# RWKV-7 scan products and second block-inverse products, issued in turn by head

## The chip, the cores and the metric

The kernel runs on one core of a Trainium2 chip. The metric is the device time of one execution in microseconds (us); lower is better. Before the change the median of three runs is 2846.87 us (2844.48 to 2854.17).

## The reference

Two layers of a hybrid generator run over 256 context and 256 latent tokens of width 2048. Each layer makes one input projection, sends it through four mixers in parallel (A: windowed attention, B: RWKV-7, C: global attention, D: gated DeltaNet), gates and merges them, and projects back. Cut to what the change touches:

```python
# the four mixers of a layer; B (RWKV-7) and D (gated DeltaNet) are the recurrent ones
p = h @ w_in;  pc = hc @ w_in
y_b, z_b = _mixer_b(p[..., OFF_B:OFF_C], pc[..., OFF_B:OFF_C], ...)
y_d, z_d = _mixer_d(p[..., OFF_D:OFF_G], pc[..., OFF_D:OFF_G], ...)
x = x + gate[:, None] * _merge([y_a, y_b, y_c, y_d], p[..., OFF_G:], g_up, g_b, w_br, w_out)

def _rwkv_scan(s0, r, w, k, v, kk, a, reverse):          # 8 heads of 64 channels, two directions
    def step(s, inp):                                    # one token
        r_t, w_t, k_t, v_t, kk_t, a_t = inp
        sa = jnp.einsum('bhij,bhj->bhi', s, -kk_t)
        s = (s * w_t[:, :, None, :] + sa[..., None] * (kk_t * a_t)[:, :, None, :]
             + v_t[..., None] * k_t[:, :, None, :])
        return s, jnp.einsum('bhij,bhj->bhi', s, r_t)
    s, y = lax.scan(step, s0, xs, reverse=reverse)

def _gdn_chunked(s0, q, k, v, lg, beta):                 # mixer D, chunks of 64 tokens
    t_mat = a_mat + jnp.eye(c)                           # unit lower triangular
    sol = lax.linalg.triangular_solve(t_mat, rhs, left_side=True, lower=True, unit_diagonal=True)
    ...
```

## The kernel before

**Tiling of the scan.** The kernel does not walk the RWKV recurrence by token. It cuts 512 tokens into eight chunks of 64 and writes a chunk's work as 64x64 matrix products in float32. Two heads are worked at a time (the loop over `j` in `mixer_b`, four pairs per layer). Head 0 of the pair lies in partitions 0 to 63, head 1 in partitions 64 to 127: `HS` in `b_scan`. A product of head 0 uses rows and columns 0 to 63 of TensorE's array and one of head 1 uses rows and columns 64 to 127. Below, a digit behind a letter is the head.

**One step of `b_scan`** (eight per direction and head pair, 128 in all) consists of, in the order of the code:

- Z: `a` = AT10 by vt and, from the second step on, `b` = ar by the state S, summed in one PSUM tile `sc`; DVE copies it to `Z`.
- U: `z` = the inverse block (tile `iR`) by Z; DVE copies it to `U`.
- S: `k` = tok1 by vt and `u` = tok0 by U, summed in one tile `sc`; DVE scales it into the new state `S` (not on the last step).
- y, where outputs are needed: `V` = vt by AT11, `s` = S by ar, `w` = U by AT01, summed in PSUM tile `acc`.

**Block inverses.** `inv_gen` inverts 64x64 unit triangular blocks. DVE solves 32x32 halves by substitution (tiles `it`, `iX`, then two transposes into `iE` and `iF`). TensorE then joins them by two sets of 32x32 products: the first set (`p1`, iF by iL) alternates between the two halves of the partitions already; the second (`p2`, iT by iE) goes through the list `out`. Each entry of `out` holds one half and four or eight blocks. It runs 24 times: 16 times for B with 16 second products, 8 times for D (`pair`) with 24.

**What sets the order.** Every matmul goes through `Kern.mm` (L283), which charges a planner's cost for it in `small`. When the debt is high enough the planner pumps the next portion of a queue of wide products into the program: input projections, modulation, merges (tiles `big`, weights `wh` and `wl` split by ACT at L375 and DVE at L312). So scan steps and wide products lie mixed on TensorE. The change alters no charged cost: a product costs by its own shape and by the form of the one before it. Last, a scheduler rearranges the recorded instructions of each engine before they become the program; TensorE then starts its list strictly in the order that stands there.

Of the kernel before, what the change touches and what calls it, by code (L numbers as in the profile page):

```python
# [187 lines left out]
class Kern:  # L188
# [515 lines left out]
    def inv_gen(s, pool, st, sign, grp, R, pair=False):  # L704

        nc = s.nc
        Bt, X, lo = st
        x = X.rearrange("p m i -> p i m")  # L710
        for k in range(31):
            n, w = 31 - k, k // 4 + 1
            tm = s.tl(pool, [128, 80], "it")[:, 0:n * w].rearrange("p (a b) -> p a b", a=n)
            b = Bt[:, k, k + 1:32].rearrange("p (a o) -> p a o", o=1).to_broadcast([128, n, w])
            s.tt(tm, b, x[:, k:k + 1, 0:w].to_broadcast([128, n, w]), ALU.mult)
            yield
            s.tt(x[:, k + 1:, 0:w], x[:, k + 1:, 0:w], tm, ALU.subtract if sign > 0 else ALU.add)
            yield
        fl = X.rearrange("p a b -> p (a b)")
        o4 = lambda z: z.rearrange("p u (m d) -> p m d u", d=4)  # L720
        E = s.tl(pool, [128, 8, 32], "iE")
        F = s.tl(pool, [128, 8, 32], "iF")
        nc.vector.transpose(o4(E), fl)
        yield
        nc.vector.transpose(F, E)

        for _ in range(6):
            yield
        ps = s.bank()
        p1 = ps[:, 0:256].rearrange("p (u c) -> p u c", u=8)  # L730
        p2 = ps[:, 256:512].rearrange("p (u c) -> p u c", u=8)
        T1 = s.tl(pool, [128, 8, 32], "iT")
        HQ = [(slice(64 * h, 64 * h + 32), slice(64 * h + 32, 64 * h + 64)) for h in range(2)]

        w = R.shape[2] - 64
        out = [(R, h, u0, u1, 0, wE) for u0, u1, wE in grp for h in range(2)]
        if pair:
            EX = s.tl(pool, [128, 4, 64], "iG")
            out += [(EX, 0, 0, 4, 0, True), (EX, 1, 4, 8, 4, False)]
        for u in range(8):  # L740
            for up, dn in HQ:
                s.mm(p1[up, u, :], lo[dn, u, :], F[dn, u, :])
        for up, dn in HQ:
            nc.scalar.copy(T1[up], p1[up])
        for D_, h, u0, u1, du, wE in out:
            up, dn = HQ[h]
            c = w * h if D_ is R else 0
            X_ = E if wE else F
            d = slice(u0 - du, u1 - du)
            nc.gpsimd.memset(D_[up, d, c + 32:c + 64] if wE else D_[dn, d, c:c + 32], 0.0)  # L750
            nc.gpsimd.tensor_copy(D_[up, d, c:c + 32], X_[up, u0:u1])
            nc.gpsimd.tensor_copy(D_[dn, d, c + 32:c + 64], X_[dn, u0:u1])
        yield
        for D_, h, u0, u1, du, wE in out:
            up, dn = HQ[h]
            for u in range(u0, u1):
                if wE:
                    s.mm(p2[dn, u, :], T1[up, u, :], E[up, u, :])
                else:
                    s.mm(p2[up, u, :], E[up, u, :], T1[up, u, :])  # L760
        for D_, h, u0, u1, du, wE in out:
            up, dn = HQ[h]
            c = w * h if D_ is R else 0
            d = slice(u0 - du, u1 - du)
            if wE:
                s.act(D_[dn, d, c:c + 32], p2[dn, u0:u1, :], AF.Copy, float(-sign))
            else:
                s.act(D_[up, d, c + 32:c + 64], p2[up, u0:u1, :], AF.Copy, float(-sign))
        if not pair:
            return  # L770
        yield
        H0, H1 = slice(0, 64), slice(64, 128)
        ps = s.bank((128, 8, 64))
        for u0, u1, wE in grp:
            f1 = EX[H1] if wE else R[H1, u0:u1, 64:128]
            for u in range(u0, u1):
                s.mm(ps[H0, u, :], R[H1, u, 0:64], f1[:, u - u0, :])
        T2 = s.tl(pool, [128, 8, 64], "iB")
        nc.scalar.copy(T2[H0], ps[H0])
        for u0, u1, wE in grp:  # L780
            nc.gpsimd.memset(R[H0, u0:u1, 64:128] if wE else R[H1, u0:u1, 0:64], 0.0)
        yield
        ps = s.bank((128, 8, 64))
        for u0, u1, wE in grp:
            for u in range(u0, u1):
                if wE:
                    s.mm(ps[H1, u, :], T2[H0, u, :], R[H0, u, 0:64])
                else:
                    s.mm(ps[H0, u, :], EX[H0, u - u0, :], T2[H0, u, :])
        for u0, u1, wE in grp:  # L790
            if wE:
                s.act(R[H1, u0:u1, 0:64], ps[H1, u0:u1, :], AF.Copy, float(-sign))
            else:
                s.act(R[H0, u0:u1, 64:128], ps[H0, u0:u1, :], AF.Copy, float(-sign))
# [176 lines left out]
    def b_scan(s, J, d):  # L971
        nc = s.nc
        pool, t0 = s.bst["pool"], s.bst["t0"]
        c0 = t0 // 64
        ar, AT, tok, E, wc = J["d"][d]
        vt = J["vt"]
        HS = (slice(0, 64), slice(64, 128))
        if d == 0:
            J["y"] = s.acc_bank()
        yps = J["y"]  # L980
        pc = None
        S = None
        for st in range(8):
            c = s.ORDER[d][st]
            ps = s.scb((128, 64))
            for R in HS:
                s.mm(ps[R, :], AT[1][0][R, c, :], vt[R, c, :], True, st == 0)
                if st > 0:
                    s.mm(ps[R, :], ar[R, c, 0, :], S[R, :], False, True)
            Z = s.tl(pool, [128, 64], "Z")  # L990
            nc.vector.tensor_copy(Z, ps)
            s.bgstep(BG[0])
            ps = s.scb((128, 64))
            for R in HS:
                s.mm(ps[R, :], E[R, c, :], Z[R, :])
            U = s.tl(pool, [128, 64], "U")
            nc.vector.tensor_copy(U, ps)
            s.bgstep(BG[1])
            Sn = None
            if st < 7:  # L1000
                ps = s.scb((128, 64))
                for R in HS:
                    s.mm(ps[R, :], tok[1][R, c, :], vt[R, c, :], True, False)
                    s.mm(ps[R, :], tok[0][R, c, :], U[R, :], False, True)
                Sn = s.tl(pool, [128, 64], "S")
                if st == 0:
                    s.ts(Sn, ps, wc[:, c:c + 1], None, ALU.mult)
                else:
                    sw = s.tl(pool, [128, 64], "sw")
                    s.act(sw, S, AF.Copy, wc[:, c:c + 1])  # L1010
                    s.stt(Sn, ps, wc[:, c:c + 1], sw, ALU.mult, ALU.add)
            if c >= c0:
                for R in HS:
                    o = yps[R, c * 64:c * 64 + 64]
                    s.mm(o, vt[R, c, :], AT[1][1][R, c, :], d == 0 and c == c0, False)
                    if st > 0:
                        s.mm(o, S[R, :], ar[R, c, 1, :], False, False)
                    s.mm(o, U[R, :], AT[0][1][R, c, :], False, d == 1 and st == 7)
            s.bgstep(BG[2])
            S = Sn  # L1020

# [579 lines left out]
```

## Time and profile before

| | |
|---|---|
| median of three runs | 2846.87 us |
| the profiled execution's own time | 2842.45 us |
| its span | 2840.7 us |
| TensorE matmul busy | 2710.4 us, 95% |
| DVE, ACT, GpSimd busy | 65%, 44%, 6% |
| TensorE's granted clock over the span | 0.984 |

An entry of the profile is one hardware instruction. A float32 product 64x64 or 32x32 leaves two matmul entries (two passes), and the entries of two products can overlap in time. The end of an entry is modelled, so the time that a stretch of small products takes is read from the start of its first entry to the start of the wide product that follows it.

### The profile page before, as it was taken

How to read it: one execution, taken by the hardware profiler on the slowest of the kernel's cores; microseconds unless marked ns; L12 is line 12 of the kernel's file. 1: busy time of each engine (PE TensorE's matmuls, PEld its weight loads, DVE VectorE, ACT ScalarE, POOL GpSimd, SP SyncE). 2: the span in 40 equal slices, each digit the busy share in tenths (PEclk: the TensorE clock that was granted, in tenths of full speed). 3: DMA queues.
4: the chain of work that ended last, by engine and by line, in shares of the span. 5: the costliest groups of instructions: out<-in, count | busy, mean ns of one | idle time of the engine just before them, and what ended most of it. 6: DMA issues, size and time to landing. Idle time of an engine off the chain costs nothing. (4 is left out here: it accounts for less than half of the span.)

```text
span 2840.7 us, 52626 instructions
## 1 busy us (share of the span) xinstructions
PE 2710.4 (95%) x19438; PEld 2056.8 (72%) x19438; DVE 1856.9 (65%) x5255; ACT 1260.0 (44%) x2705; POOL 180.0 (6%) x436
## 2 busy tenths in 40 slices
PE   7998999999999998999999999999999999999897
PEld 3676666677787786777787756776777887867897
DVE  4337776656676777876553354777765687678775
ACT  3334333333354555655442244444443356455553
POOL 0000000000010101000000000010010001100000
PEclk9999999999999999999999999999999999999999
DMA  9753243322342323224537886322332442433465
GB/s 346 261 189 127 83 131 105 127 83 68 115 121 88 100 72 115 79 82 134 170 114 248 279 282 203 96 78 78 93 91 75 157 143 88 133 98 88 144 190 159
DMA packets 210049, 385.80 MB, mean 136 GB/s; under 512 B 24640, under 2 KB 37824, under 8 KB 209792
## 3 DMA queue, kind: packets, MB, share of 16 engines
q1 hardware_dynamic: 199872, 351.23, 39.6%
q0 software_dynamic: 9920, 31.20, 2.9%
q8 instruction: 153, 2.51, 0.4%
q14 instruction: 104, 0.85, 0.1%
HBM read 346.95 MB, written 35.39 MB: 135 GB/s over the span
## 5 line engine op out<-in xcount | busy, mean ns | idle before, releaser
L283 PE MATMUL big<-Rb,wh 128*128 128x512 f32 (+1 forms) x3280 | 1100.7, 364 | 21.3 <-ACT Rb L1325 10.0
L283 PE MATMUL big<-Ra,wh 128*128 128x512 f32 (+1 forms) x2128 | 777.3, 365 | 8.9 <-DVE po L315 5.6
L375 ACT CAST wh<-wr 128x512 fp32r<-128x512 f32 x712 | 438.8, 619 | 762.8 <-PE big L283 576.2
L283 PEld LDWEIGHTS big<-Rb,wh 128*128 128x128 f32 x3280 | 612.1, 191 | 128.8 <-ACT Rb L1325 14.0
L312 DVE TENSOR_TENSOR wl<-wr,wh 128x512 fp32r<-128x512 f32 x712 | 488.4, 688 | 304.3 <-ACT wh L375 280.3
L283 PE MATMUL big<-Ra,wl 128*128 128x512 f32 (+1 forms) x1616 | 597.2, 370 | 6.3 <-DVE wl L312 6.3
L283 PEld LDWEIGHTS big<-Ra,wh 128*128 128x128 f32 x2128 | 407.5, 192 | 84.3 <-issue 9.5
L283 PE MATMUL big<-Rb,wl 128*128 128x512 f32 (+1 forms) x1088 | 380.4, 350 | 1.1 <-DVE wl L312 1.1
L283 PEld LDWEIGHTS big<-Ra,wl 128*128 128x128 f32 x1616 | 310.3, 192 | 53.4 <-DVE wl L312 8.6
L283 PEld LDWEIGHTS big<-Rb,wl 128*128 128x128 f32 x1088 | 207.6, 191 | 26.2 <-DVE wl L312 1.5
L312 DVE TENSOR_TENSOR iX<-iX,it 128x60 f32<-128x60 f32 (+24 forms) x744 | 181.4, 244 | 15.7
L312 DVE TENSOR_TENSOR it<-iB,iX 128x60 f32<-128x60 f32 (+24 forms) x744 | 172.7, 232 | 15.6
L315 DVE SCALAR_TENSOR_TENSOR po<-po,big 128x512 f32<-128x512 f32 (+1 forms) x128 | 70.6, 552 | 77.1 <-PE big L283 74.2
L283 PE MATMUL big<-Rb,wr 128*128 128x256 f32 (+1 forms) x448 | 111.3, 417 | 5.0 <-ACT po L309 3.1
L309 ACT ACTIVATE sw<-S,wc 128x64 f32<-128x64 f32 x96 | 33.4, 348 | 176.2 <-DVE S L315 153.5
L283 PE MATMUL big<-mr,s 128*32 128x512 f32 x384 | 85.2, 617 | 18.3 <-DMA mr<-in_wmod 18.3
L309 ACT ACTIVATE po<-big,gb 128x512 f32<-128x512 f32 (+1 forms) x128 | 74.2, 579 | 57.3 <-PE big L283 41.2
L283 PEld LDWEIGHTS big<-Rb,wr 128*128 128x128 f32 (+1 forms) x448 | 70.6, 179 | 24.1 <-issue 7.3
L283 PE MATMUL sc<-vt,AT 64*64 64x64 f32 x512 | 71.3, 238 | 0.0
L315 DVE SCALAR_TENSOR_TENSOR cz<-raw,par,cz 128x508 f32<-128x508 f32 (+3 forms) x96 | 67.2, 700 | 5.4 <-ACT cz L309 5.0
L632 DVE TENSOR_REDUCE mx<-mx 128x1 f32<-128x512 f32 (+1 forms) x96 | 57.1, 599 | 18.7 <-PE mx L283 17.5
L283 PE MATMUL sc<-vt,tok 64*64 64x64 f32 x448 | 67.5, 232 | 0.0
(371 smaller groups left out, 4033.0 us busy)
## 6 DMA issues: line engine op xcount, KB each, us to landing
wr<-in_win SPq DMA_DIRECT2D x440, 256.0 KB, 2.7
mr<-in_wmod SPq DMA_DIRECT2D x320, 256.0 KB, 5.0
wr<-in_wbr SPq DMA_DIRECT2D x128, 256.0 KB, 2.7
wr<-in_wout SPq DMA_DIRECT2D x128, 256.0 KB, 3.1
wr<-in_wmod SPq DMA_DIRECT2D x64, 256.0 KB, 3.9
wr<-in_gup SPq DMA_DIRECT2D x64, 256.0 KB, 2.6
x<-in_xT SPq DMA_DIRECT2D x16, 256.0 KB, 5.4
po<-y SPq DMA_DIRECT2D x16, 256.0 KB, 3.0
```

The lines of the kernel that those rows point to most:

```text
L283: s.nc.tensor.matmul(o, l, r, start=start, stop=stop)
L309: s.nc.scalar.activation(o, i, f, bias=bias, scale=scale, **k)
L312: s.nc.vector.tensor_tensor(o, a, b, op)
L315: s.nc.vector.scalar_tensor_tensor(o, a, sc, b, op0, op1)
L375: s.nc.scalar.copy(hi, raw)
L632: nc.vector.tensor_reduce(mx[:, hc], ps[:, 0:nk], AX.X, ALU.max)
```

## The change

In the second set of products of `inv_gen` the entries of `out` are sorted by half, and the products of the two halves are then issued in turn, one of each. In `b_scan` every loop over the heads that held two or three products is split into loops with one product each, so the heads alternate product by product. No product is added or removed, and no operand, destination or accumulation flag changes.

```diff
--- before.py
+++ after.py
@@ -751,9 +751,10 @@
             nc.gpsimd.tensor_copy(D_[up, d, c:c + 32], X_[up, u0:u1])
             nc.gpsimd.tensor_copy(D_[dn, d, c + 32:c + 64], X_[dn, u0:u1])
         yield
-        for D_, h, u0, u1, du, wE in out:
-            up, dn = HQ[h]
-            for u in range(u0, u1):
+
+        a, b = [[(u, wE) for _, g, u0, u1, _, wE in out if g == h for u in range(u0, u1)] for h in range(2)]
+        for z in zip(a, b):
+            for (up, dn), (u, wE) in zip(HQ, z):
                 if wE:
                     s.mm(p2[dn, u, :], T1[up, u, :], E[up, u, :])
                 else:
@@ -985,6 +986,7 @@
             ps = s.scb((128, 64))
             for R in HS:
                 s.mm(ps[R, :], AT[1][0][R, c, :], vt[R, c, :], True, st == 0)
+            for R in HS:
                 if st > 0:
                     s.mm(ps[R, :], ar[R, c, 0, :], S[R, :], False, True)
             Z = s.tl(pool, [128, 64], "Z")
@@ -1001,6 +1003,7 @@
                 ps = s.scb((128, 64))
                 for R in HS:
                     s.mm(ps[R, :], tok[1][R, c, :], vt[R, c, :], True, False)
+                for R in HS:
                     s.mm(ps[R, :], tok[0][R, c, :], U[R, :], False, True)
                 Sn = s.tl(pool, [128, 64], "S")
                 if st == 0:
@@ -1010,12 +1013,14 @@
                     s.act(sw, S, AF.Copy, wc[:, c:c + 1])
                     s.stt(Sn, ps, wc[:, c:c + 1], sw, ALU.mult, ALU.add)
             if c >= c0:
+                o = lambda R: yps[R, c * 64:c * 64 + 64]
                 for R in HS:
-                    o = yps[R, c * 64:c * 64 + 64]
-                    s.mm(o, vt[R, c, :], AT[1][1][R, c, :], d == 0 and c == c0, False)
-                    if st > 0:
-                        s.mm(o, S[R, :], ar[R, c, 1, :], False, False)
-                    s.mm(o, U[R, :], AT[0][1][R, c, :], False, d == 1 and st == 7)
+                    s.mm(o(R), vt[R, c, :], AT[1][1][R, c, :], d == 0 and c == c0, False)
+                if st > 0:
+                    for R in HS:
+                        s.mm(o(R), S[R, :], ar[R, c, 1, :], False, False)
+                for R in HS:
+                    s.mm(o(R), U[R, :], AT[0][1][R, c, :], False, d == 1 and st == 7)
             s.bgstep(BG[2])
             S = Sn
```

How TensorE's program reads at one step of the first scan (layer 0). Each row is one product, written as out<-in,in by tile name; x2 stands for two equal names in succession, here always head 0 and then head 1. The head of a lone row does not show in it and is given in the text behind. Before:

```order
L283 MATMUL sc_594_2600<-vt_437_1919,tok1_480_2116 64x64
L283 MATMUL big_605_2637<-Ra_359_1560,wh_673_2889 128x512
L283 MATMUL big_605_2637<-Rb_360_1561,wh_673_2889 128x512
L283 MATMUL sc_594_2600<-U_592_2594,tok0_478_2106 64x64
L283 MATMUL sc_594_2600<-vt_437_1919,tok1_480_2116 64x64
L283 MATMUL sc_594_2600<-U_592_2594,tok0_478_2106 64x64
L283 MATMUL acc_570_2519<-AT01_455_1999,U_592_2594 64x64
L283 MATMUL acc_570_2519<-AT11_464_2044,vt_437_1919 64x64
L283 MATMUL acc_570_2519<-ar_445_1943,S_584_2567 64x64
L283 MATMUL acc_570_2519<-AT01_455_1999,U_592_2594 64x64
L283 MATMUL sc_599_2621<-vt_437_1919,AT10_463_2043 64x64
L283 MATMUL acc_570_2519<-AT11_464_2044,vt_437_1919 64x64
```

After:

```order
L283 MATMUL sc_594_2600<-vt_437_1919,tok1_480_2116 64x64 x2
L283 MATMUL big_605_2637<-Ra_359_1560,wh_673_2889 128x512
L283 MATMUL big_605_2637<-Rb_360_1561,wh_673_2889 128x512
L283 MATMUL sc_594_2600<-U_592_2594,tok0_478_2106 64x64 x2
L283 MATMUL acc_570_2519<-AT01_455_1999,U_592_2594 64x64 x2
L283 MATMUL sc_599_2621<-vt_437_1919,AT10_463_2043 64x64 x2
L283 MATMUL acc_570_2519<-AT11_464_2044,vt_437_1919 64x64 x2
```

Ahead of the two wide products stood z1 k0; now z1 k0 k1 stands there. The stretch behind them went from u0 k1 u1 w0 V1 s1 w1 a0 V0 to u0 u1 w0 w1 a0 a1 V0 V1; s1 moved to an earlier stretch.

A later step of the same layer, with all six products of y behind the state. Before:

```order
L283 MATMUL sc_967_4186<-vt_715_3104,tok1_756_3298 64x64
L283 MATMUL sc_967_4186<-U_965_4180,tok0_754_3288 64x64
L283 MATMUL sc_967_4186<-vt_715_3104,tok1_756_3298 64x64
L283 MATMUL sc_967_4186<-U_965_4180,tok0_754_3288 64x64
L283 MATMUL acc_939_4095<-AT11_747_3242,vt_715_3104 64x64
L283 MATMUL acc_939_4095<-ar_723_3128,S_948_4120 64x64
L283 MATMUL acc_939_4095<-AT01_734_3187,U_965_4180 64x64
L283 MATMUL acc_939_4095<-AT11_747_3242,vt_715_3104 64x64
L283 MATMUL acc_939_4095<-ar_723_3128,S_948_4120 64x64
L283 MATMUL acc_939_4095<-AT01_734_3187,U_965_4180 64x64
L283 MATMUL sc_972_4207<-vt_715_3104,AT10_746_3241 64x64
L283 MATMUL acc_939_4095<-AT11_747_3242,vt_715_3104 64x64
```

After:

```order
L283 MATMUL sc_967_4186<-vt_715_3104,tok1_756_3298 64x64 x2
L283 MATMUL sc_967_4186<-U_965_4180,tok0_754_3288 64x64 x2
L283 MATMUL acc_939_4095<-AT11_747_3242,vt_715_3104 64x64 x2
L283 MATMUL acc_939_4095<-ar_723_3128,S_948_4120 64x64 x2
L283 MATMUL acc_939_4095<-AT01_734_3187,U_965_4180 64x64 x2
L283 MATMUL sc_972_4207<-vt_715_3104,AT10_746_3241 64x64 x2
L283 MATMUL sc_972_4207<-S_968_4191,ar_723_3128 64x64 x2
L283 MATMUL acc_939_4095<-AT11_747_3242,vt_715_3104 64x64 x2
L283 MATMUL acc_939_4095<-ar_723_3128,S_968_4191 64x64 x2
```

Before, the order was k0 u0 k1 u1 V0 s0 w0 V1 s1 w1 a0 V0, a wide product, b0 a1 and on. Now it runs k0 k1 u0 u1 V0 V1 s0 s1 w0 w1 a0 a1 b0 b1 and the next V and s in nine pairs, and the wide product stands behind them.

The order of the whole TensorE program beside these places is nearly kept: of its 14480 products, 88 stand more than 15 places from where they stood, most of them the `V` of a second head. In the 32x32 products of the inverse the rows read alike before and after, since their names do not show the half.

## Rows read from the trace of the kernel before

**Rows 1.** Page, part 1: busy time, share, instructions.

```profile
PE 2710.4 (95%) x19438; PEld 2056.8 (72%) x19438; DVE 1856.9 (65%) x5255; ACT 1260.0 (44%) x2705; POOL 180.0 (6%) x436
```

**Rows 2.** Stretches: length, busy per engine (instructions), TensorE clock, DMA share, GB/s.

```profile
230.00:530.00 300.00, 287.37 (x2715) 195.08 (x2715) 210.38 (x647) 114.93 (x257) 21.59 (x48) 0.99 0.36 116
530.00:790.00 260.00, 257.38 (x2153) 189.07 (x2148) 165.94 (x493) 86.33 (x180) 20.12 (x39) 0.99 0.29 89
...
900.00:1240.00 340.00, 321.88 (x1980) 251.72 (x1981) 266.89 (x803) 199.28 (x471) 31.70 (x83) 0.98 0.31 94
...
1800.00:2000.00 200.00, 192.81 (x1960) 142.30 (x1958) 147.26 (x500) 87.11 (x197) 17.40 (x38) 0.95 0.27 81
2000.00:2205.00 205.00, 202.37 (x2013) 153.77 (x2011) 137.09 (x459) 81.50 (x183) 17.83 (x40) 1.00 0.30 87
```

**Rows 3.** Waits of TensorE: total us, times, longest.

```profile
PE mx L283 <- DVE iF L725: 18.6, 8, 4.7
...
PE sc L283 <- DVE Z L991: 0.9, 1, 0.9
...
PE sc L283 <- DVE U L997: 0.5, 2, 0.3
PE sc L283 <- DVE S L315: 0.4, 1, 0.4
```

**Rows 4.** Timeline of TensorE, one step: start, length, operation, count.

```profile
285.67 0.32 PE L283 MATMUL sc<-Z,iR 64*64 64x64 f32 x2
285.93 0.66 PE L305 MATMUL mx<-cst,E 128*128 128x128 f32 x4
286.51 0.27 PE L283 MATMUL sc<-Z,iR 64*64 64x64 f32 x1
286.52 0.27 PE L283 MATMUL sc<-vt,tok 64*64 64x64 f32 x1
...
286.78 0.50 PE L283 MATMUL big<-Ra,wh 128*128 128x512 f32 x1
...
287.44 0.27 PE L283 MATMUL sc<-U,tok 64*64 64x64 f32 x1
287.44 0.27 PE L283 MATMUL sc<-vt,tok 64*64 64x64 f32 x1
...
288.22 0.49 PE L283 MATMUL big<-Ra,wl 128*128 128x512 f32 x1
...
289.62 0.27 PE L283 MATMUL sc<-S,ar 64*64 64x64 f32 x1
...
290.00 1.06 PE L283 MATMUL big<-wr,s 128*32 128x512 f32 x6
```

**Rows 5.** Timeline around one block inverse.

```profile
269.98 0.69 PE L283 MATMUL mx<-iF,iL 32*32 32x32 f32 x32
270.60 0.50 PE L283 MATMUL mx<-was,lorh 128*128 128x512 f32 x1
...
271.73 1.09 PE L283 MATMUL mx<-iT,iE 32*32 32x32 f32 x32
...
272.75 0.50 PE L283 MATMUL big<-Ra,wh 128*128 128x512 f32 x1
```

**Rows 6.** Timeline of a step without a wide product behind it.

```profile
549.45 0.22 PE L283 MATMUL sc<-U,tok 64*64 64x64 f32 x1
...
549.71 0.28 DVE L315 SCALAR_TENSOR_TENSOR S<-sc,wc,sw 128x64 f32<-128x64 f32 x1 [0.45 <-PE sc L283]
...
550.05 0.27 PE L283 MATMUL sc<-S,ar 64*64 64x64 f32 x1
```

**Rows 7.** Page, part 5: the split of weights on DVE.

```profile
L312 DVE TENSOR_TENSOR wl<-wr,wh 128x512 fp32r<-128x512 f32 x712 | 488.4, 688 | 304.3 <-ACT wh L375 280.3
```

## The prediction

> **What bounds the kernel now.** I read the busy shares first, then the stretches, then TensorE's waits, and last the timeline of single steps. TensorE has matmuls in flight 95% of the span, no other engine is busy over 65% [rows 1]. The RWKV scans lie from 230 to 790 us (layer 0) and from 1800 to 2205 us (layer 1). In these 965 us TensorE has matmuls in flight for 940 (287.4 + 257.4 + 192.8 + 202.4), while DVE is busy 0.64 to 0.74 of each stretch and the DMA engines 0.27 to 0.36 [rows 2]. The scan is a chain over DVE (Z, U, S), but the planner lays wide products between its links: all waits for Z, U and S together that the list of waits shows are 1.8 us [rows 3]. So the length of the scan stages is the length of TensorE's list, and a change is worth what it takes out of that list.
>
> **How small products are paid for.** The timeline shows it directly. The stretch with z0 alone takes 0.26 us to the start of the next wide group (285.67 to 285.93); the stretch z1 k0, two products of different halves, takes 0.27 (286.51 to 286.78) [rows 4]. So a product of the other half rides along free. b0 a1 b1 s0 takes 0.38 (289.62 to 290.00), and u0 k1 u1 w0 V1 s1 w1 a0 V0 takes 0.78 (287.44 to 288.22) [rows 4]. I call a turn the time in which each half can work off one product; products start in list order, and one of a half waits for the last one of the same half. By that count the four stretches have 1, 1, 2 and 6 turns: (0.38 - 0.27)/1 = 0.11 and (0.78 - 0.27)/5 = 0.10 a turn. I take 0.11 us a turn on top of about 0.15 for entering and leaving a stretch.
>
> For 32x32 products the two sets of one inverse stand side by side: 16 products, alternating, take 0.62 us (269.98 to 270.60), and 16 with eight of one half and then eight of the other 1.02 (271.73 to 272.75) [rows 5]. That is 8 turns against 15, since only the last of one half meets the first of the other: (1.02 - 0.62)/7 = 0.057 us a turn.
>
> **The change part by part.** It adds and removes no instruction, DMA or byte; it only reorders. I count turns over the whole lists of before and after.
>
> The scan: the program has 446 stretches of 64x64 products with 1604 turns before, 441 with 1396 after. Not every step gains. The commonest stretch, z0 z1 k0 (97 times, 2 turns), becomes z0 z1 k0 k1 and still has 2. b0 a1 b1 (44 times, 2 turns) becomes b0 b1 (1 turn). The long stretch of nine (25 times, 6 turns) becomes eight products in 4, and its sister without the last V0 (23 times, 5 turns) becomes one of 3. The saving is less than half of the turns, because the scheduler had already put heads against each other with one product of offset. 208 turns by 0.11 = 22.9 us.
>
> The inverses: stretches of 32x32 products go from 595 to 429 turns (a whole second set of 16 from 15 to 8, one of 24 from 19 to 12). 166 turns by 0.057 = 9.5 us. Of these, 111 turns lie in the scan stages of B and 55, or 3.1 us, in D's.
>
> Six stretches fewer (446 to 441, and 77 to 76) by 0.15 = 0.9 us. Sum: 22.9 + 9.5 + 0.9 = 33.3 us.
>
> **What of it is not kept.** In the D stages TensorE is at 95% of the stretch [rows 2], and it waited 8 times, 18.6 us in all, for the transposes that end DVE's substitution [rows 3]. Time saved ahead of such a wait is lost; I write off half of D's 3.1 us, 1.6. In the scans the links have to keep their cover. The tightest kind is a step without wide products: the last pass of u1 starts at 549.45 and ends at 549.67, DVE forms S from 549.71 for 0.28 us, and b0 starts at 550.05 [rows 6]. The link itself needs about 0.38 us (0.04 + 0.28 + 0.06) and the y products behind u1 were its cover. They now pass in about two turns, 0.22 us, less. Most links have wide products in their cover; for some ten in which this wait opens I take off 0.1 us each, 1.0 in all. Below zero this can't go by much: the wait before b0 and u0 used to hold up a1 and k1 too, and these now stand ahead of it. So 33.3 - 2.6 = 30.7, about 31 us.
>
> The profiled execution took 2842.45 us, 1.8 more than its span; it would take 2811.5. It lies 4.4 under the median of the runs, 2846.87; from the median I forecast 2816 us. The forecast's own range: at 0.10 a turn with all of D's share lost and 4 us of new waits, 20.8 + 6.3 + 0.9 - 4 = 24 us; at 0.12 a turn (0.38 against 0.26) and nothing lost, 25.0 + 9.5 + 0.9 = 35.4, and some 4 us for instructions that the scheduler moved elsewhere: 2807 to 2825.
>
> **A rule that speaks against it.** At 287.44 us the first passes of u0 and k1 start within 0.01 us, each 0.27 long [rows 4]; by the order of instructions both write the same PSUM tile, in different partitions. The Trainium skill ("TensorEngine Tiling (Array Packing)", Restrictions and Gotchas, the gotcha on PSUM pressure) says that different row tiles must write to different PSUM banks and cannot use one bank at the same time. By that rule the alternating pairs (z0 z1, u0 u1, V0 V1) would pass one after the other and the scan would gain nothing. The trace does not agree with it here.
>
> **The rivals.**
> - Half is lost to what paces TensorE behind it. If the list gets 3% shorter in the scans, the wide products ask sooner for split weights: DVE needs 0.69 us for each [rows 7] and takes its work in order, in between Z, U, S and the substitution. For it speaks DVE's 0.74 in 1800 to 2000 us, and that every S link loses cover: 112 links by 0.22 us would be 25 us at the worst. Against it speaks 1.8 us of waits now. Half of 31 kept: 2831 us.
> - Pairs that write one PSUM tile don't overlap, so that only the few stretches less are gained: 0.9 us, 2846. For it speaks nothing in these rows; against it z1 k0 and u0 k1 in [rows 4] and the alternating set in [rows 5].
> - Slower. DVE takes work in order. If the earlier asked-for weights put a whole split of 0.69 us [rows 7] in front of the state's update in each of the 112 S links, TensorE stands 77 us longer, net of the gain 46: 2893. It decides from 31/112 = 0.28 us a link on. Against it: DVE has a quarter of its time free, and wide products stand in most links.
> - More than the sum. Where TensorE already waits in a link, shorter product groups bring Z and U earlier as well, and the inverse's second set ends 0.4 us sooner on the way to the scan. If a tenth of the 25 us in which TensorE was idle in the scan stages (965 - 940) went and nothing were lost elsewhere, with 0.12 a turn, it is 35 + 3, and with the scheduler's moves some 45: 2802.
>
> **How the numbers follow.** Chances: forecast 0.74, half lost 0.13, no overlap 0.04, slower 0.04, more 0.05. A measurement of this kernel tells 0.3%, 8.5 us, from no change: faster is below 2838.3. Forecast, more, and 0.10 of the half-lost case are faster: 0.89. The rest of that case, no overlap and 0.01 of the slower case are within the bound: 0.08. Slower: 0.03. The range goes from 2800 (most of the case of more) to 2836 (most of half lost).
>
> **What would show it.** In the profile after, u0 and u1, V0 and V1 start within 0.01 us of each other; the eight-product stretch takes about 0.58 us (0.78 less two turns) and b0 b1 about 0.27; the second set of an inverse takes about 0.62 us from its first entry to the next wide product, as the first set does. The stretch of layer 0's scans should be about 16 us shorter (122 and 55 turns), layer 1's 13 (86 and 56), each D stage under 2. Waits of TensorE for Z, U and S should stay under some 5 us. The prediction is wrong if second products of a pair start one turn after the first, or if the turns go and the waits for DVE grow by as much.

## The result and the profile after

The changed kernel takes 2817.95 us (median of four runs, 2813.9 to 2822.62) against 2845.68 for the kernel before in the same series; the ratio is 0.9897, interval 0.9871 to 0.9922. A second series of five against fifteen runs gave 0.9892 (0.9875 to 0.9909). The forecast was 2816 us.

The page's first part, beside [rows 1]: TensorE's time with matmuls in flight falls by 16.6 us and that with weight loads (PEld) by 21.5; the other engines stay within 2 us.

```profile
PE 2693.8 (96%) x19438; PEld 2035.3 (72%) x19438; DVE 1855.0 (66%) x5255; ACT 1259.1 (45%) x2705; POOL 180.8 (6%) x436
```

The timeline of TensorE at the same step as [rows 4] (start, length, operation; entries of one name that overlap are merged and counted, two to a product):

```profile
289.80 0.27 PE L283 MATMUL sc<-Z,iR 64*64 64x64 f32 x1
289.81 0.27 PE L283 MATMUL sc<-vt,tok 64*64 64x64 f32 x1
289.91 0.22 PE L283 MATMUL sc<-Z,iR 64*64 64x64 f32 x1
289.92 0.33 PE L283 MATMUL sc<-vt,tok 64*64 64x64 f32 x3
290.18 0.50 PE L283 MATMUL big<-Ra,wh 128*128 128x512 f32 x1
290.51 0.40 PE L283 MATMUL big<-Rb,wh 128*128 128x512 f32 x1
290.84 0.33 PE L283 MATMUL sc<-U,tok 64*64 64x64 f32 x4
291.00 0.28 PE L283 MATMUL acc<-AT,U 64*64 64x64 f32 x4
291.12 0.28 PE L283 MATMUL sc<-vt,AT 64*64 64x64 f32 x4
291.24 0.28 PE L283 MATMUL acc<-AT,vt 64*64 64x64 f32 x4
291.45 0.50 PE L283 MATMUL big<-Ra,wl 128*128 128x512 f32 x1
...
292.86 0.33 PE L283 MATMUL sc<-S,ar 64*64 64x64 f32 x4
293.02 0.28 PE L283 MATMUL acc<-ar,S 64*64 64x64 f32 x4
293.24 0.63 PE L283 MATMUL big<-wr,s 128*32 128x512 f32 x3
```

Each pair now takes one turn: u0 u1 start at 290.84, w0 w1 at 291.00, a0 a1 at 291.12, V0 V1 at 291.24, so 0.16 us behind the first pair and 0.12 behind each later one. The stretch lasts 0.61 us (290.84 to 291.45) where it had 0.78. The stretch z1 k0 k1 is now 0.38 long instead of 0.27: this is where the step pays for k1, which before stood behind u0.

The inverse of [rows 5]: the second set takes 0.63 us to the next wide product, where it took 1.02.

```profile
273.46 0.69 PE L283 MATMUL mx<-iF,iL 32*32 32x32 f32 x32
274.08 0.50 PE L283 MATMUL mx<-was,lorh 128*128 128x512 f32 x1
...
275.20 0.69 PE L283 MATMUL mx<-iT,iE 32*32 32x32 f32 x32
275.83 0.50 PE L283 MATMUL big<-Ra,wh 128*128 128x512 f32 x1
```

Waits of TensorE (total us, times, longest), beside [rows 3]: no new wait of any size.

```profile
PE mx L283 <- DVE iF L725: 20.7, 9, 5.1
...
PE sc L283 <- DVE Z L993: 1.6, 1, 1.6
...
PE sc L283 <- DVE U L999: 0.6, 2, 0.3
...
PE sc L283 <- DVE S L315: 0.3, 1, 0.3
```

Where the time went: I cut both executions at the same instructions, the first product with the weights of the decay (tile `was`) and the last with Z of each layer. The columns are the stretch, its length, busy time of TensorE, of its weight loads, DVE, ACT and GpSimd, TensorE's granted clock, DMA share and GB/s. Before:

```profile
227.50:734.80 507.30, 493.31 (x4621) 342.64 (x4621) 334.54 (x1054) 180.72 (x400) 34.09 (x76) 0.99 0.32 101
734.80:1768.80 1034.00, 1002.34 (x5440) 759.25 (x5440) 651.35 (x1644) 485.92 (x1020) 55.83 (x137) 0.99 0.47 150
1768.80:2202.50 433.70, 423.01 (x4186) 320.28 (x4184) 310.02 (x1031) 185.62 (x418) 36.86 (x81) 0.98 0.29 85
2202.50:2840.70 638.20, 588.46 (x4292) 509.87 (x4292) 470.81 (x1356) 326.22 (x724) 44.65 (x121) 0.97 0.44 133
```

After:

```profile
232.00:723.90 491.90, 480.68 (x4628) 330.35 (x4626) 333.98 (x1055) 180.91 (x400) 33.98 (x76) 0.99 0.33 104
723.90:1754.90 1031.00, 1002.78 (x5434) 758.54 (x5434) 651.27 (x1643) 485.62 (x1020) 56.03 (x137) 0.99 0.47 150
1754.90:2176.10 421.20, 410.48 (x4188) 307.70 (x4185) 308.76 (x1031) 185.31 (x418) 37.57 (x81) 0.98 0.29 87
2176.10:2817.90 641.80, 592.48 (x4291) 512.72 (x4289) 470.98 (x1356) 326.03 (x724) 44.65 (x121) 0.95 0.44 132
```

The scan stages give 15.4 and 12.5 us, the stretch from there to layer 1's scans, which holds layer 0's D stage, gives 3.0. The stretch ahead of the first scan, which the change doesn't touch, is 4.5 us longer (227.5 to 232.0) at a granted clock of 0.98 against 1.00, and the last stretch 3.6 us longer at 0.95 against 0.97. So the two profiles differ by no more than 22.8 us, and the clocks differ the same way: the profiled execution of before had 0.984 over its span, that of after 0.977. Over all runs of the second series the two kernels have the same clock, 0.979 in the mean, and there the ratio of 0.9892 makes 31 us.

### The profile page after: what moved, and what is told of

The parts are those of the page before. It is cut to its first block, busy times and chain, and to the rows that moved or that the text cites. A ratio compares the mean times of both kernels' runs of the same rounds, so it can differ in the third digit from the quotient of the medians.

```text
span 2817.9 us, 52627 instructions
## 1 busy us (share of the span) xinstructions
PE 2693.8 (96%) x19438; PEld 2035.3 (72%) x19438; DVE 1855.0 (66%) x5255; ACT 1259.1 (45%) x2705; POOL 180.8 (6%) x436
## 5 line engine op out<-in xcount | busy, mean ns | idle before, releaser
L999 DVE COPY U<-sc 128x64 f32<-128x64 f32 x128 | 28.5, 223 | 50.1 <-PE sc L283 48.8
L283 PE MATMUL mx<-pT,avt 128*64 128x128 f32 x640 | 60.5, 288 | 0.8 <-ACT pT L658 0.5
```

The costliest lines, as they stand in the source:

```text
L283: s.nc.tensor.matmul(o, l, r, start=start, stop=stop)
```

## The experiments

All times are medians; each kernel was compared with the kernel before on the same chip. "Turns" are counted in each program's order as in the prediction.

**The changed kernel again** (e0).

> The changed kernel again, beside the kernel before. Theory (turns): 208 turns of 64x64 and 166 of 32x32 fewer, about 31 us less: ratio 0.988 to 0.991. Rival (the gain of the first measurement was partly chance of the clock): ratio moves by more than 0.004 from 0.9897, and the granted clock of the runs moves with it.

Measured: 2815.69 us against 2848.3, ratio 0.9892 (0.9875 to 0.9909), clock 0.977 to 0.982. The result stands.

**The inverses alone** (e2): `inv_gen` of after, `b_scan` of before.

```diff
-        for D_, h, u0, u1, du, wE in out:
-            up, dn = HQ[h]
-            for u in range(u0, u1):
+        a, b = [[(u, wE) for _, g, u0, u1, _, wE in out if g == h for u in range(u0, u1)] for h in range(2)]
+        for z in zip(a, b):
+            for (up, dn), (u, wE) in zip(HQ, z):
```

> Only the second products of the inverses alternate; b_scan as before. Turns: 64x64 1604 as before, 32x32 595 to 430. Theory (turns): 165 by 0.057, 9.4 us less at most, 8 with half of D's share lost, about 2838. Rival (inverse products lie off the path, hidden behind DVE's substitution): 0 to 2 us less.

Measured: 2837.93 against 2848.3, ratio 0.9967 (0.9955 to 0.9979), 9.4 us less by the ratio. The turns give 9.4. So the products of the inverses are not hidden behind DVE's substitution.

**The y products by head again** (e4), the rest of the change kept.

```diff
-                o = lambda R: yps[R, c * 64:c * 64 + 64]
                 for R in HS:
-                    s.mm(o(R), vt[R, c, :], AT[1][1][R, c, :], d == 0 and c == c0, False)
...
+                    o = yps[R, c * 64:c * 64 + 64]
+                    s.mm(o, vt[R, c, :], AT[1][1][R, c, :], d == 0 and c == c0, False)
+                    if st > 0:
+                        s.mm(o, S[R, :], ar[R, c, 1, :], False, False)
+                    s.mm(o, U[R, :], AT[0][1][R, c, :], False, d == 1 and st == 7)
```

> The changed kernel, but the three y products (V, s, w) go by head as before; Z, U, S and the inverses alternate. Turns: 64x64 1505 in 444 stretches, 32x32 429 in 74. Theory (turns): 99 by 0.11, 166 by 0.057, 5 stretches by 0.15, 21 us less, some 2 lost: about 2827. Rival (what counts is that U and S are ready a turn earlier, the y products being only filling): as much as the whole change, 28 us less or more, about 2818.

Measured: 2828.74, ratio 0.9937 (0.9923 to 0.9951), 18 us less. 19 were expected by turns, 28 by the rival. So the gain is in the turns of all products, the y products among them, and not in an earlier U or S.

**The scan alone** (e1, and again on another chip as e1b): the changed kernel with the inverses' products as before.

```diff
-        a, b = [[(u, wE) for _, g, u0, u1, _, wE in out if g == h for u in range(u0, u1)] for h in range(2)]
-        for z in zip(a, b):
-            for (up, dn), (u, wE) in zip(HQ, z):
+        for D_, h, u0, u1, du, wE in out:
+            up, dn = HQ[h]
+            for u in range(u0, u1):
```

> Only b_scan alternates; the second products of the inverses go by half as before. Turns counted in its program: 64x64 1604 to 1396 in 441 stretches, 32x32 595 to 594. Theory (turns): 208 by 0.11 and 5 stretches by 0.15, 23.6 us less than before, so about 2823 from 2846. Rival (the inverses on the way to the scan give most): under 10 us less.

Measured: 2834.66, ratio 0.9955 (0.9939 to 0.997): 13 us less, where the turns give 23.6. This was a miss by 10 us, and the clock moved with it: its eight runs have 0.972 to 0.980, 0.975 in the mean, against 0.979 for the kernel before. Within these eight runs time follows clock: 2825.2 us at 0.980, 2841.82 at 0.972, about 2 us for 0.001. At 0.979 they would be near 2827, 21 less than before.

> The scan-only kernel again, since it gave 10 us less than its turns. Theory (turns and clock): its turns save about 22 us at the granted clock of the kernel before, but its clock is lower (0.975 against 0.979), so ratio 0.995 to 0.996 again with a clock of 0.974 to 0.977. Rival (an accident of the first eight runs): about 2825, ratio 0.992, clock as before.

Measured: 2834.74, ratio 0.9949 (0.993 to 0.9967), clock 0.974 to 0.980 with a mean of 0.9755; before had 0.979 on this chip too. So it is no accident: this kernel loses some 8 us to the clock.

**Which inverses the clock goes with** (e6, e7): the changed kernel, but all second products of one half and then all of the other, in D's inverses or in B's.

```diff
-        for z in zip(a, b):
-            for (up, dn), (u, wE) in zip(HQ, z):
+        order = [(h, z[h]) for z in zip(a, b) for h in range(2)]
+        if pair:                      # e7: if not pair
+            order = [(h, q) for h in range(2) for q in (a, b)[h]]
+        if True:
+            for h, (u, wE) in order:
+                up, dn = HQ[h]
```

> The changed kernel, but the inverses of mixer D issue all second products of one half and then all of the other; B's alternate. Turns of 32x32: 516 against 429. Theory (turns): 87 by 0.057, 5 us more than the changed kernel at most, about 2820, granted clock as in the changed kernel. Rival (D's inverses are what lowers the clock of the scan-only kernel): clock 0.975 and about 2830.

Measured: 2822.98 against 2847.87, ratio 0.991 (0.9893 to 0.9928), mean clock 0.978. By the ratios that is 5 us over the changed kernel, as the turns say, and the clock stays nearly where it was.

> The changed kernel, but the inverses of mixer B issue all second products of one half and then all of the other; D's alternate. Turns of 32x32: 539 against 429. Theory (turns alone): 110 by 0.057, 6 us more than the changed kernel, about 2822, clock 0.979. Theory (turns and clock): B's stretches of one half let the clock fall more often in the scans, clock 0.975 and 2828 to 2834.

Measured: 2831.36, ratio 0.9939 (0.992 to 0.9958), clock 0.973 to 0.978 with a mean of 0.9757. By the ratios that is 13 us over the changed kernel, where the turns alone say 6. The other 7 go with the clock: it is 0.003 below the changed kernel's 0.979, at about 2 us for 0.001. Around three inverses of B in layer 1, stretches of 20 us of this kernel:

```profile
1843.00:1863.00 20.00, 19.36 (x159) 13.55 (x157) 10.53 (x37) 7.70 (x19) 2.86 (x6) 0.74 0.15 47
1894.00:1914.00 20.00, 18.53 (x157) 15.96 (x157) 13.21 (x42) 9.59 (x19) 3.44 (x7) 0.83 0.36 109
1948.00:1968.00 20.00, 19.34 (x175) 8.98 (x174) 10.01 (x35) 7.57 (x17) 2.51 (x6) 0.83 0.16 47
```

the same three inverses in the second profile of the changed kernel:

```profile
1831.00:1851.00 20.00, 19.37 (x193) 13.16 (x192) 14.32 (x45) 9.16 (x22) 2.86 (x6) 1.00 0.23 60
1880.00:1900.00 20.00, 18.34 (x234) 15.31 (x234) 15.80 (x43) 13.52 (x29) 3.99 (x8) 1.00 0.49 150
1931.00:1951.00 20.00, 19.34 (x254) 11.19 (x247) 12.35 (x35) 10.08 (x24) 3.00 (x7) 1.00 0.19 61
```

and in the kernel before, whose second sets in B also go one half after the other:

```profile
1851.00:1871.00 20.00, 19.59 (x166) 14.08 (x165) 11.87 (x40) 8.86 (x21) 2.87 (x6) 0.83 0.16 50
1902.00:1922.00 20.00, 18.44 (x202) 15.55 (x201) 15.67 (x48) 11.58 (x23) 4.01 (x8) 1.00 0.42 121
1956.00:1976.00 20.00, 19.83 (x226) 10.32 (x227) 12.80 (x39) 9.04 (x21) 3.06 (x7) 1.00 0.17 60
```

TensorE's matmul entries cover 18.3 of 20 us and more in all nine, yet in e7 the clock fell to its lower level (1.2 GHz) within each of its three. A fall is neither certain with half-wise sets (the kernel before has one in three) nor ruled out without them: the first profile of the changed kernel has 0.83 around the first of these inverses. So e1 and e7 show that kernels with the scan's products in turn and B's sets by half run at a lower mean clock; what makes the clock fall is not shown. It remains open too why the kernel before, which has the same half-wise sets beside slower scan steps, keeps 0.979.

**More turns instead of fewer** (e3): the products of `b_stage1`, which alternated before and after, put head by head in the changed kernel.

```diff
-        for c in range(8):
-            for h in range(2):
+        for h in range(2):
+            for c in range(8):
...
-                for cc in range(4):
-                    c = 4 * g + cc
-                    for h in range(2):
+                for h in range(2):
+                    for cc in range(4):
+                        c = 4 * g + cc
```

> The changed kernel, but the products that prepare a scan (b_stage1), which alternated already, go by head: eight or four of head 0, then of head 1. Turns of 64x64: 1627 against 1396, more than before the change (1604). Theory (turns): 231 by 0.11, 25 us more than the changed kernel, about 2841. Rival (long stretches of small products are limited by something else than turns, such as weight loads): under 10 us more.

Measured: 2837.14 against 2847.87, ratio 0.9965 (0.9951 to 0.9978): 21 us more than the changed kernel, at a clock of 0.980. A set of 32 products that took 2.01 us in 16 turns (changed kernel, first fence) takes 2.97 in 27 (this one). That is 0.09 us a turn within the set; over the whole kernel 21 us for 231 turns, 0.09 too. So more turns cost time about as fewer give it back.

```profile
395.17 2.08 PE L283 MATMUL mx<-ar,th 64*64 64x64 f32 x64
397.18 0.50 PE L283 MATMUL big<-Ra,wl 128*128 128x512 f32 x1
```

```profile
394.75 3.04 PE L283 MATMUL mx<-ar,th 64*64 64x64 f32 x64
397.72 0.50 PE L283 MATMUL big<-Ra,wl 128*128 128x512 f32 x1
```

**What a turn is bound to** (e5): the last set of 64x64 products of D's inverses, all from partitions 0 to 63, four to 64 to 127 and four to 0 to 63, in turn by the half that is written.

```diff
-        for u0, u1, wE in grp:
-            for u in range(u0, u1):
+        for z in zip(*[[(u, u - u0, wE) for u in range(u0, u1)] for u0, u1, wE in grp]):
+            for u, v, wE in z:
...
-                    s.mm(ps[H0, u, :], EX[H0, u - u0, :], T2[H0, u, :])
+                    s.mm(ps[H0, u, :], EX[H0, v, :], T2[H0, u, :])
```

> The changed kernel; in addition the last set of 64x64 products of D's inverses (eight products, all reading partitions 0 to 63, four writing partitions 64 to 127 and four 0 to 63) alternates by the half that is written. Theory (turns go by the half that is read): still 8 turns, the set keeps its length of about 1 us, time as the changed kernel within 2 us. Rival (a turn is taken only by products that also write the same half): 4 turns fewer in each of 8 inverses, 32 by 0.11, 3.5 us less, each set about 0.6 us long.

Measured: 2815.88 against 2849.77, ratio 0.9878 (0.9858 to 0.9898); the time can't be told from the changed kernel's, but the set can. Timeline of the changed kernel, then of this one:

```profile
879.21 0.50 PE L283 MATMUL mx<-iB,iG 64*64 64x64 f32 x5
...
880.10 0.50 PE L283 MATMUL big<-Ra,wl 128*128 128x512 f32 x1
```

```profile
879.79 0.27 PE L283 MATMUL mx<-iB,iG 64*64 64x64 f32 x1
879.80 0.27 PE L283 MATMUL mx<-iR,iB 64*64 64x64 f32 x1
...
880.40 0.50 PE L283 MATMUL big<-Ra,wl 128*128 128x512 f32 x1
```

0.89 us became 0.61 by three turns (the last product of one kind and the first of the other overlapped already). My theory was wrong here: two products that read the same half and write different halves overlap as well. So sharing the rows of the array does not cost a turn. Whether sharing the columns does, with different rows, no run here shows: nowhere do two neighbouring 64x64 products read different halves and write the same one. For the scan's products, where the half read is the half written, the counts are the same.

## Why the prediction was right

- **TensorE's list sets the scan stages.** Right: layer 0's stage lost 15.4 us (16 said), layer 1's 12.5 (13 said). The stretch that holds layer 0's D stage lost 3.0, where under 2 was said for a D stage.
- **The price of a turn.** Right: pairs start together, the stretch of eight takes 0.61 (0.58 said), the second set of an inverse 0.63 (0.62 said). Summed over all their stretches in the two profiles, from the first entry to the next form's first, the 64x64 products went from 265.5 to 244.0 us, 21.5 where 22.9 and 0.75 for stretches were said; the 32x32 products from 48.1 to 38.6, 9.5 as said. Inverses alone (e2) and y products by head (e4) gave 9.4 and 18 us, 9.4 and 19 by turns.
- **The order of starts.** Not as said. The prediction and the section on the kernel before have TensorE start its products strictly in list order. In the stretch of nine of [rows 4] the list ends V1 s1 w1 a0 V0, but a0 (`sc<-vt,AT`) starts with s1, 0.11 us before w1 (`acc<-AT,U`):

```profile
287.84 0.22 PE L283 MATMUL acc<-ar,S 64*64 64x64 f32 x1
287.85 0.27 PE L283 MATMUL sc<-vt,AT 64*64 64x64 f32 x1
...
287.96 0.22 PE L283 MATMUL acc<-AT,U 64*64 64x64 f32 x1
288.01 0.22 PE L283 MATMUL acc<-AT,vt 64*64 64x64 f32 x1
```

So a product whose half is free can start ahead of one that waits for its own half, and the stretch of nine is less than six full turns. After the change the stretches of one to five turns take 0.26, 0.38, 0.50, 0.61 and 0.73 us (medians), 0.117 a turn; six of these would be 0.85 us, not 0.78. The price of 0.10 to 0.11 came out low where the strict count came out high, and their product was nearly right: 208 turns gave 21.5 us, 0.10 each.

- **What is not kept.** The waits for Z and U rose from 1.4 to 2.2 us, the waits for iF from 18.6 to 20.7. 2.6 us were set aside for such losses. But the stretches had given 31.0 us (21.5 and 9.5), not 33.3, and the runs got 31 us faster: the count too high and the loss set aside nearly cancel, which is luck, and the runs' interval is too wide to tell the two apart. Of the 18.6 us before, 5.1 lay in layer 1's scan stage and not in D's. DVE didn't become late, and neither the half-lost nor the slower rival occurred.
- **Two sums.** The least gain of the forecast's own range, 24 us, ends at 2823 and not 2825; the case of more adds up to 42 us (35.4, 2.5 and 4), about 2805, and not 45. Neither touches the forecast.
- **Pairs in one PSUM tile.** They overlap: u0 and u1 write one `sc` tile, start within 0.01 us of each other, and their pair takes one turn. The gotcha on PSUM pressure of the Trainium skill's page "TensorEngine Tiling (Array Packing)" (Restrictions and Gotchas) is not borne out for two halves of the partitions of one tile.
- **What the sum left out.** The clock was given no term. For the whole change it needed none, since its mean is 0.979 on both sides. But this was luck of the combination: the scan part without B's inverse part lost about 7 to 8 us with it (e1, e1b, e7). A forecast for the scan alone would have missed by 10 us.

## What to carry to other kernels

Count small products in turns. Here a product rode along free beside one that used another quarter of the array and wrote other partitions, and one of the same quarter cost a turn, about 0.12 us for 64x64 and 0.06 for 32x32 in float32. 16 products of 32x32 took 0.63 us in turn and 1.02 one half after the other. Count them in the order that the scheduler leaves, not in the code's: here it had already put many products side by side (2576 products of 64x64 took 1604 turns), and the change could only win the rest. Check the count of a long mixed stretch against its time in the trace, for some products start ahead of their place in the list. And compare the granted clock of the runs before reading a few us out of two profiles: two single profiles were off by 8 us of 31.

## What the runs showed that was not expected

- TensorE's clock can fall while its matmul entries cover the stretch: 0.74 over 20 us with 19.36 us busy (e7). That stretch holds an inverse whose second set goes one half after the other, but no run shows that this set is the cause.
- About 2 us go with each 0.001 of the mean clock in this kernel (e1's runs), and the runs of one kernel, the one before, spread over 0.975 to 0.984.
- Two 64x64 products that read the same partitions overlap if they write different ones: 8 in 0.61 us against 0.89 (e5).
- TensorE does not always start products in list order: a0 started 0.11 us before w1, which stands ahead of it, in the step of [rows 4], and so it did in all 25 stretches of nine of the kernel before.
